# Hymba layer on one core: SyncE's requests for the MLP's rows move ahead of the writes of the block before

## The chip, the core and the metric

The kernel runs on one core of a Trainium2 chip. The metric is the device time of one execution in microseconds (us); the time before is the median of three runs. All work is in float32, with matmul operands split in a high and a low part (three products stand for one). TensorE (PE) multiplies and transposes, VectorE (DVE) and ScalarE (ACT) do elementwise work and empty PSUM, GpSimd (POOL) does small work and issues some transfers, SyncE (SP) issues most transfers. Each engine works through its own list in order; a SyncE instruction that has to wait for data or for a free buffer holds up what stands behind it in SyncE's list.

## The reference

One layer of a decoder: two mixers side by side (sliding-window attention and a gated short convolution) and then an MLP with a squared ReLU. 2048 positions, width 1024, MLP width 4096.

```python
h = rms_norm(x, attn_norm_g[l])
z = h @ w_in[l]                       # q, k, v, gate_b, gate_c, xc by columns
y_attn = swa_sink_attention(rms_norm(q, q_norm_g[l]), rms_norm(k, k_norm_g[l]), v, sinks[l])
y_conv = gate_b * short_conv(gate_c * xc, conv_w[l])
y = concatenate([rms_norm(y_attn, attn_out_g[l]), rms_norm(y_conv, conv_out_g[l])])
x = x + y @ w_out[l]
hm = rms_norm(x, mlp_norm_g[l])
x = x + square(relu(hm @ w_up[l])) @ w_down[l]
```

## The kernel before

**Stages.** The mixers run over four chunks of 512 positions (`NCHUNK`, chunk 0 to 3); each chunk's result, the rows x1, is stored to `x1_dram` (L1027). The MLP follows, with its up product (L1514) and its down product (L1631). Both of the MLP's products are done by a scheme of seven block products in place of eight (`ORDER`), which needs sums and differences of blocks of the input. These are the seven planes `xop_dram` that `x_put` (L326 and following) writes.

**The blocks.** The first half of the positions (chunks 0 and 1) is made ready for the MLP while TensorE still works on the last chunk's convolution. This is `x_blocks`. It has `NT` = 4 blocks. Block `t` holds two tiles of 128 rows by 1024 columns: rows of chunk 0 and the same rows of chunk 1. For each block SyncE requests both tiles from `x1_dram` (L351). After three pauses (`X_WAIT`), ScalarE scales a tile by its norm (L357), TensorE transposes it in two halves (L363) through the only PSUM bank with the tag "tr", and VectorE empties the bank with the gain (L364), back into the same tile. Three of the resulting four pieces are written out as they are (L373, the write itself at L334). Four differences are then made in place by VectorE (L377), each over a piece that an earlier write or difference still reads, and each is written too (L378). That is seven writes of 256 KB for a block, against two requests of 512 KB.

**The buffers.** The eight tiles take turns in buffers of the mixers: block 0 the two "xt", block 1 "gb" and one "x1", block 2 two "x1", block 3 one "x1" and again the first "xt". The four "x1" buffers hold the rows of chunk 2 before, and those of chunk 3 (loaded at L1056) afterwards. "gb" holds a gain row of the attention's norm until the last chunk's input is made.

**The order of the work.** `x_blocks` is a generator. `besides` goes one pause further in it at every second step of `conv_pair` (`X_EVERY`), so a block's 12 pauses are spread over the convolution's products. The program order so written is not yet an engine's order: a planner ranks all instructions by their place in the program, shifted in places by `tc.high_priority(offset=...)` (here `ahead(12)` and `ahead(13)`), and simulates the program; each engine takes, of the instructions that are ready at a moment of that simulation, the one that ranks first. An instruction that needs a buffer is ready when the buffer is free in the simulation. `tc.issue_after` pins the transposes behind the latest product. The engine lists that come out of it are fixed when the kernel is built.

Of the kernel before, what the change touches and what calls it, by code (L numbers as in the profile page):

```python
# [36 lines left out]
NT = CH // P  # L37
# [57 lines left out]
def hymba_layer(  # L95
# [50 lines left out]
    def bank(tag, name):  # L146
        return psum.tile([P, 512], F32, tag=tag, name=name, bufs=BANKS[tag])

    def row(tag, name, bufs, dt=F32):

        return pool.tile([P, D], dt, tag=tag, name=name, bufs=bufs)
# [35 lines left out]
    def ahead(i):  # L187

        offset = PRIO[stage[0]][i]
        return tc.high_priority(offset=offset) if offset else nullcontext()  # L190
# [137 lines left out]
    def x_put(tb, t, i, b):  # L328

        dst = xop_dram[tb][ORDER.index(i)]  # L330
        if tb:
            nc.sync.dma_start(dst[:, t * BW : (t + 1) * BW], b)
        else:
            nc.sync.dma_start(  # L334
                dst.rearrange("p (h t c) -> p h t c", h=2, t=NB)[:, :, t], b.rearrange("p (h c) -> p h c", h=2)
            )

    def rs_out(c):

        nc.gpsimd.dma_start(  # L340
            rs_dram[c].rearrange("(p t) -> p t", p=P), rs_x1[:, c * NT : (c + 1) * NT]
        )

    def x_blocks():

        for t in range(NT):
            tags = (("xt", 2), ("xt", 2), ("gb", 1), *((("x1", NT),) * 4), ("xt", 2))[2 * t : 2 * t + 2]
            rows = [row(tag, f"xt_m{c}_{t}", bufs) for c, (tag, bufs) in enumerate(tags)]
            for c, xt in enumerate(rows):
                r = (c * NT + t) * P  # L350
                nc.sync.dma_start(xt, x1_dram[r : r + P, :])  # L351
            for _ in range(X_WAIT):
                yield
            for c, xt in enumerate(rows):
                r = c * NT + t
                with ahead(12):
                    nc.scalar.activation(xt, xt, AF.Copy, scale=rs_x1[:, r : r + 1])  # L357
                for k in range(2):
                    with ahead(12), tc.issue_after(last_sum[0]):
                        pt = bank("tr", f"pt_m{c}_{t}_{k}").rearrange("p (j q) -> p j q", j=NB)  # L360
                        b = xt[:, k * BW : (k + 1) * BW]
                        for j in range(NB):
                            nc.tensor.transpose(pt[:, j], b[:, j * P : (j + 1) * P], ident)  # L363
                        nc.vector.tensor_tensor(  # L364
                            b.rearrange("p (j q) -> p j q", j=NB),
                            pt,
                            g_cols[:, k * NB : (k + 1) * NB, None].to_broadcast([P, NB, P]),
                            op=ALU.mult,
                        )
                    yield  # L370
            b11, b21, b12, b22 = (xt[:, k * BW : (k + 1) * BW] for xt in rows for k in range(2))
            for i, b in ((3, b22), (1, b11), (2, b21)):
                x_put(0, t, i, b)  # L373
            yield
            for i, dst, a, b in ((5, b11, b12, b11), (7, b12, b22, b12), (6, b22, b22, b11), (4, b21, b21, b22)):
                with ahead(13):
                    nc.vector.tensor_tensor(dst, a, b, op=ALU.subtract)  # L377
                    x_put(0, t, i, dst)  # L378
                yield

    def merged(dst, *planes):

        pairs = dst.bitcast(U16).rearrange("p k (t i) -> p i k t", i=2)
        for i, plane in enumerate(planes):
            nc.vector.tensor_copy(pairs[:, i], plane)
# [9 lines left out]
    def prepare(src, r0, gb, dst, name):  # L395
# [29 lines left out]
        def whole(t):  # L425
            with ahead(9), behind():
                for n, raw in enumerate(places[t]):
                    merged(
                        raw.rearrange("p (k t) -> p k t", k=KH), *(turned_[t][:, i, n * KH : (n + 1) * KH] for i in range(2))
                    )  # L430
# [245 lines left out]
    with tc.tile_pool(name="mix_small", bufs=1) as mix_small, tc.tile_pool(name="mix", bufs=1) as mix:  # L676
# [60 lines left out]
        def qk_transpose(b, zt):  # L737

            nm = f"b{b}"
            own = b % 2  # L740
            lo, hi = slice(0, DH), slice(DH, P)
            sc = mix.tile([P, HEADS, P], F32, tag="sc", name=f"sc_{nm}", bufs=2) if b >= TURN_Q else None
            qt = mix.tile([P, HEADS // 2, 2, P], F32R, tag="qt", name=f"qt_{nm}", bufs=1)
            if b >= TURN_Q:
                turned_z = zt[:, :O_V].bitcast(U16).rearrange("p (i n t) -> p i n t", i=2, t=P)
                with ahead_z(2):
                    merged(sc[:, : O_V // P], turned_z[:, 0], turned_z[:, 1])
                p3, pk = sc[:, :4], sc[:, 4]
            else:
                pt = bank("at", f"ptq_{nm}")  # L750
                for j in range(4):
                    nc.tensor.transpose(pt[:, j * P : (j + 1) * P], zt[:, j * P : (j + 1) * P], ident)
                pk = bank("at", f"ptk_{nm}")[:, :P]
                nc.tensor.transpose(pk, zt[:, O_K:O_V], ident)
                p3 = pt.rearrange("p (j q) -> p j q", j=4)
            for i, (a, o) in enumerate(((lo, hi), (hi, lo))):
                nc.scalar.copy(qt[a, :, i, :], p3[a])
                nc.vector.tensor_tensor(qt[o, :, i, :], p3[a], qt[a, :, i, :].bitcast(F32), op=ALU.subtract)
                nc.scalar.copy(kw[a, i, i, own, :], pk[a])
                nc.scalar.copy(kw[o, 1 - i, i, own, :], pk[a])  # L760
                nc.vector.tensor_tensor(kw[o, i, i, own, :], pk[a], kw[a, i, i, own, :].bitcast(F32), op=ALU.subtract)
                nc.vector.tensor_tensor(
                    kw[a, 1 - i, i, own, :], pk[a], kw[a, i, i, own, :].bitcast(F32), op=ALU.subtract
                )
            return qt, sc
# [217 lines left out]
        def out_projection(c, half, ys, rs, x1):  # L983

            for dh in range(2):
# [11 lines left out]
                for t, i in order:  # L997
# [21 lines left out]
                    with ahead(11):  # L1019
                        nc.vector.scalar_tensor_tensor(  # L1020
                            x1[t][:, cs], ps, rs[:, t : t + 1], x1[t][:, cs], op0=ALU.mult, op1=ALU.add
                        )
                        if dh and not half:
                            r = (c * NT + t) * P

                            eng = nc.gpsimd if c + 1 == NCHUNK else nc.sync
                            eng.dma_start(x1_dram[r : r + P, :], x1[t])  # L1027

                            if c + 1 < NCHUNK:
                                norm_stats(x1[t], f"m{c}_{t}", rs_x1[:, c * NT + t : c * NT + t + 1])  # L1030
                                if t + 1 == NT and c == NCHUNK - 2:
                                    rs_out(c)
                    yield

        def besides(c, before, h, yt, rc, x1, h_next, z_next):

            yield from before
            ssc = mix.tile([P, CH], F32, tag="ssc", name=f"ssc{c}", bufs=1)
            blocks = x_blocks() if c + 1 == NCHUNK else None
            if c + 1 < NCHUNK:  # L1040
                steps = prepare(xf, (c + 1) * CH, g_row[0], h_next, f"a{c + 1}")
# [263 lines left out]
    def prepare_rest():  # L1305

        c = NCHUNK - 1
        for t in range(NT):
# [4 lines left out]
            norm_stats(xt, nm, rs_x1[:, r // P : r // P + 1], junk=piece("st", f"junk_{nm}"))  # L1313
            yield
        rs_out(c)
        rows = pool.tile([P, 2, BW], F32, tag="xt", name="rs_rest", bufs=2)
        for i in range(2):
# [353 lines left out]
```

## Time and profile before

| What | Value |
|---|---|
| Time, median of 3 runs | 1910.71 us (1909.95 to 1911.93) |
| Profiled execution's own time | 1909.29 us |
| Its span, first to last instruction | 1907.6 us |
| TensorE busy | 1895.1 us (99%) |
| VectorE busy | 1230.1 us (64%) |
| ScalarE busy | 868.5 us (46%) |
| HBM read and written | 286.35 MB and 125.83 MB |
| Requests of the blocks (L351) | 8 transfers, 468.8 to 569.1 us |
| Writes of the blocks (L334) | 28 transfers, 553.1 to 636.6 us |
| Transposes of the blocks (L363) | 64, 550.5 to 626.8 us |

Times inside the profile are counted from the start of the span. A row of a timeline gives the start, the length, the engine, the line of the kernel, the operation with output and input, the number of instructions merged in it, and in brackets the engine's idle time before it and what ended that. "SPq" is SyncE's queue of transfers. In a table of stretches each engine has its busy time and number of instructions, and at the end stand the granted clock of TensorE, the busy share of the DMA engines and the rate in GB/s. The span and the launch around it differ by 1.69 us in the profiled execution.

### The profile page before, as it was taken

The numbers are of one execution on the slowest core, as the hardware profiler recorded it, in microseconds if no ns is written. First come the engines' busy times: TensorE is split into PE (matmuls) and PEld (weight loads), VectorE is DVE, ScalarE is ACT, GpSimd is POOL, SyncE is SP. The second block draws the span as 40 slices with busy tenths as digits, with TensorE's granted clock in tenths as the row PEclk, the third lists the DMA queues.
The fourth block names the chain that finished last, engine by engine and source line by source line (L and its number), as shares of the span: only waits on it lengthen the run. The fifth ranks groups of instructions, "written<-read, shape, count | busy, mean of one in ns | idle before, by whom it ended". The sixth has DMA issues, their size and how long they took to land.

```text
span 1907.6 us, 24456 instructions
## 1 busy us (share of the span) xinstructions
PE 1895.1 (99%) x8774; PEld 1574.3 (83%) x8774; DVE 1230.1 (64%) x1929; ACT 868.5 (46%) x1605; POOL 291.2 (15%) x477
## 2 busy tenths in 40 slices
PE   9999999999999999999999999999999999999999
PEld 8878887888877888888888888888888888888887
DVE  5886577568568759998788766666534334447441
ACT  6656356456554445545565545463322232222220
POOL 2213213322221112233111101011000000100000
PEclk9999999999999999999999999999999999999999
DMA  8997965667687688777575544448954456776541
GB/s 294 336 293 200 330 243 198 213 241 233 206 304 254 225 295 250 230 211 248 201 242 197 176 140 161 138 155 320 367 194 144 144 168 225 280 230 210 186 158 55
DMA packets 273690, 424.03 MB, mean 222 GB/s; under 512 B 92568, under 2 KB 177312, under 8 KB 260768
## 3 DMA queue, kind: packets, MB, share of 16 engines
q1 hardware_dynamic: 244736, 346.82, 55.5%
q0 software_dynamic: 15424, 51.40, 6.9%
q10 hardware_dynamic: 13408, 24.26, 3.4%
q8 instruction: 69, 1.13, 0.2%
q14 instruction: 53, 0.43, 0.1%
HBM read 286.35 MB, written 125.83 MB: 216 GB/s over the span
## 4 chain that ended last, share of the span: by engine, by line
PE 47%; issue 5%; POOL 1%; DMA 0%; DVE 0%; DVEq 0%; POOLq 0%
PE d L1631 32%; PE u L1514 15%; POOL fop L1250 1%; DMA fop<-s 0%; POOL st_m L1188 0%; DVE wop L492 0%; DVE d L1574 0%; DVE op_x L473 0%; POOLq L1250 0%; DVEq L1666 0%; DVE s L1253 0%; DVEq L1253 0%; DVEq L492 0%; DVEq L473 0%
## 5 line engine op out<-in xcount | busy, mean ns | idle before, releaser
L1514 PE MATMUL u<-op_x,wop 128*128 128x512 f32 x2688 | 609.8, 389 | 0.5 <-DVE wop L492 0.5
L1631 PE MATMUL d<-op_w,op_f 128*128 128x512 f32 x2691 | 609.5, 389 | 0.0
L1514 PEld LDWEIGHTS u<-op_x,wop 128*128 128x128 f32 x2688 | 504.3, 188 | 105.8 <-DVE wop L492 0.9
L1631 PEld LDWEIGHTS d<-op_w,op_f 128*128 128x128 f32 x2691 | 504.8, 188 | 104.7
L473 DVE TENSOR_TENSOR op_f<-op_f 128x1024 fp32r<-128x1024 f32 x112 | 136.9, 1225 | 236.7 <-ACT op_f L472 236.5
L472 ACT CAST op_f<-op_f 128x1024 fp32r<-128x1024 f32 x112 | 117.7, 1052 | 354.1 <-DMA op_f<-fop 341.0
L491 ACT CAST wop<-wu 128x512 fp32r<-128x512 f32 x156 | 96.1, 619 | 89.1 <-PE u L1514 86.7
L492 DVE TENSOR_TENSOR wop<-wu,wop 128x512 fp32r<-128x512 f32 x156 | 110.4, 710 | 31.4 <-DMA wu<-in_w_up_dram 20.1
L1250 POOL DMA_DIRECT2D fop<-s x96 | 52.1, 542 | 443.5 <-DVE s L1253 439.1
L1256 DVE TENSOR_TENSOR u<-u,u 128x512 f32<-128x512 f32 x128 | 87.9, 687 | 18.6 <-PE u L1514 18.3
L473 DVE TENSOR_TENSOR op_w<-raw,op_w 128x1024 fp32r<-128x1024 f32 x56 | 68.3, 1222 | 23.6 <-ACT op_w L472 23.4
L472 ACT CAST op_w<-raw 128x1024 fp32r<-128x1024 f32 x56 | 58.8, 1052 | 44.0 <-DVE raw L1461 20.3
L828 POOL TENSOR_SCALAR_AFFINE_SELECT pp_b<-pp_b 128x512 fp32r<-128x512 f32 x60 | 46.5, 785 | 140.3 <-ACT pp_b L821 86.9
L1262 ACT ACTIVATE u<-u 128x512 f32<-128x512 f32 x64 | 40.5, 632 | 58.6 <-DVE u L1256 56.3
L796 ACT ACTIVATE sc_b<-sc_b,ngm_b 128x128 f32<-128x128 f32 x128 | 49.6, 389 | 22.6 <-DVE ngm_b L793 22.5
L1463 POOL DMA_DIRECT2D wds<-raw x16 | 8.5, 533 | 329.3 <-DVE raw L1461 329.3
L492 DVE TENSOR_TENSOR wop<-wu_s,wop 128x512 fp32r<-128x512 f32 x64 | 46.0, 720 | 11.9 <-ACT wop L491 11.8
L491 ACT CAST wop<-wu_s 128x512 fp32r<-128x512 f32 x64 | 39.4, 619 | 30.2 <-PE u L1514 24.5
L281 PE MATMUL pout<-w_wo,yt_c 128*128 128x512 f32 x128 | 50.7, 397 | 0.8 <-DVE x L1020 0.7
L281 PE MATMUL pb_c<-h_a,w_wb 128*128 128x512 f32 x128 | 51.2, 400 | 0.0
L282 PE MATMUL pout<-w_wo,yt_c 128*128 128x512 f32 x128 | 50.6, 396 | 0.4 <-DVE w_wo L254 0.4
L281 PE MATMUL pc_c<-h_a,w_wc 128*128 128x512 f32 x128 | 50.9, 398 | 0.1
(249 smaller groups left out, 3141.5 us busy)
## 6 DMA issues: line engine op xcount, KB each, us to landing
op_f<-fop SPq DMA_DIRECT2D x112, 512.0 KB, 4.3
raw<-in_w_down_dram SPq DMA_DIRECT2D x72, 512.0 KB, 4.3
wu<-in_w_up_dram SPq DMA_DIRECT2D x128, 256.0 KB, 4.3
w_wo<-wo SPq DMA_DIRECT2D x24, 1024.0 KB, 7.3
fop<-s POOLq DMA_DIRECT2D x96, 256.0 KB, 2.7
fop<-u ACTq DMA_DIRECT2D x64, 256.0 KB, 2.4
op_x<-xop SPq DMA_DIRECT2D x28, 512.0 KB, 6.3
w_q<-q SPq DMA_DIRECT2D x12, 1024.0 KB, 5.6
```

Of the source, the lines that this page charges most:

```text
L281: nc.tensor.matmul(ps, st(0), mv(0), start=first, stop=False)
L282: nc.tensor.matmul(ps, st(0), mv(1), start=False, stop=False)
L472: nc.scalar.copy(op[:, 0], raw)
L473: nc.vector.tensor_tensor(op[:, 1], raw, op[:, 0].bitcast(F32), op=ALU.subtract)
L491: splits.append(nc.scalar.copy(hi, blk).ins)
L492: lows.append(nc.vector.tensor_tensor(lo, blk, hi.bitcast(F32), op=ALU.subtract).ins)
L796: nc.scalar.activation(sc[:, hd, :], sc[:, hd, :], AF.Exp, bias=ngm[:, hd : hd + 1], accum_out=den[:, hd : hd + 1])
L828: nc.gpsimd.affine_select(part, full, pattern=[[0, GQ], [1, P]], compare_op=ALU.is_ge, fill=0.0, base=0, channel_multiplier=-1,)
L1250: eng.dma_start(fop_dram[tb][ORDER_DOWN.index(i)][n // 2][:, n % 2], b)
L1256: return nc.vector.tensor_tensor(dst, ps, b, op=ALU.add).ins
L1514: nc.tensor.matmul(pt, wops[i][:, a, k, :], xops[tb, p][k // 2][:, b, k % 2, :], start=p not in GOES_ON and k + j == 0, stop=k + j == NB + ...
L1631: nc.tensor.matmul(ps[tb][j][:, cs], fs[tb][:, a, k, j * P : (j + 1) * P], w[:, b, k, cs], start=first and p not in GOES_ON and k + n == 0 ...
```

## The change

The request of a block becomes a function, `request(t)`. Block 0's is made before the loop. In block `t`, when its first tile is turned and before its second tile is scaled, the request of block `t + 1` is written; the block's seven writes come after it in the program. Before, the request of block `t + 1` stood after block `t`'s last write. What a block requests, its tags, its buffers and its pauses stay. Two more lines of the diff remove empty lines.

```diff
     def x_blocks():
-
-        for t in range(NT):
+        def request(t):
             tags = (("xt", 2), ("xt", 2), ("gb", 1), *((("x1", NT),) * 4), ("xt", 2))[2 * t : 2 * t + 2]
             rows = [row(tag, f"xt_m{c}_{t}", bufs) for c, (tag, bufs) in enumerate(tags)]
             for c, xt in enumerate(rows):
                 r = (c * NT + t) * P
                 nc.sync.dma_start(xt, x1_dram[r : r + P, :])
+            return rows
+
+        ahead_rows = request(0)
+        for t in range(NT):
+            rows = ahead_rows
             for _ in range(X_WAIT):
                 yield
             for c, xt in enumerate(rows):
+                if c and t + 1 < NT:
+                    ahead_rows = request(t + 1)
                 r = c * NT + t
                 with ahead(12):
                     nc.scalar.activation(xt, xt, AF.Copy, scale=rs_x1[:, r : r + 1])
...
```

## The prediction

> **What bounds the kernel now.** I read the page's first part for the engine that sets the end, then TensorE's busy time stage by stage, to see how much a better order could win at all.
>
> ```profile
> span 1907.6 us, 24456 instructions
> PE 1895.1 (99%) x8774; PEld 1574.3 (83%) x8774; DVE 1230.1 (64%) x1929; ACT 868.5 (46%) x1605; POOL 291.2 (15%) x477
> ...
> core 0: us, PE busy (x) PEld busy (x) DVE busy (x) ACT busy (x) POOL busy (x), PEclk, DMA share, GB/s
> 543.00:561.00 18.00, 17.43 (x99) 14.37 (x98) 10.88 (x26) 14.32 (x40) 3.68 (x10) 1.00 1.03 347
> 561.00:593.00 32.00, 29.95 (x157) 24.57 (x156) 29.92 (x71) 20.88 (x63) 6.49 (x10) 1.00 0.74 264
> 593.00:626.00 33.00, 32.64 (x165) 27.05 (x164) 27.21 (x56) 11.99 (x33) 4.92 (x8) 1.00 0.81 274
> ...
> 640.00:700.00 60.00, 60.00 (x276) 49.68 (x275) 33.45 (x53) 20.23 (x34) 9.21 (x26) 1.00 0.74 251
> 700.00:1000.00 300.00, 300.00 (x1325) 248.40 (x1324) 260.78 (x372) 166.94 (x277) 67.34 (x90) 1.00 0.74 233
> ```
>
> TensorE is idle for 1907.6 - 1895.1 = 12.5 us of the whole span, at a granted clock of 1.00. The blocks that the change touches are turned between 543 and 626 us. There TensorE is idle for 18.00 - 17.43 = 0.57, 32.00 - 29.95 = 2.05 and 33.00 - 32.64 = 0.36 us: 2.98 us together. From 640 to 1000 us it is never idle, so nothing that these blocks hand on to the MLP is late at present. What the change can win on TensorE's idle time is at most 2.98 us, 0.16% of the time.
>
> Next I read SyncE's queue in order of time, for the requests (L351) and the writes (L334). A row may hold several transfers in a row; its second number then includes the waits between them.
>
> ```profile
> start us, us, engine line op out<-in xcount [idle before <-releaser]
> 468.81 0.33 SPq L351 DMA_DIRECT2D xt_m<-x_dram  x1
> ...
> 487.61 0.32 SPq L351 DMA_DIRECT2D xt_m<-x_dram  x1
> ...
> 547.34 0.57 SPq L1027 DMA_DIRECT2D x_dram<-x  x1
> 548.02 0.38 SPq L351 DMA_DIRECT2D xt_m<-x_dram  x1
> 548.82 1.87 SPq L242 DMA_DIRECT2D w_wb<-wb  x2
> 553.14 2.80 SPq L334 DMA_DIRECT2D xop<-xt_m  x2
> 556.03 1.16 SPq L351 DMA_DIRECT2D xt_m<-x_dram  x2
> 558.52 3.76 SPq L334 DMA_DIRECT2D xop<-xt_m  x3
> ...
> 565.16 2.24 SPq L334 DMA_DIRECT2D xop<-xt_m  x2
> ...
> 568.14 1.26 SPq L351 DMA_DIRECT2D xt_m<-x_dram  x2
> ...
> 576.34 2.38 SPq L334 DMA_DIRECT2D xop<-xt_m  x2
> ```
>
> This is the view that decides for me. Each block has two rows, so the requests come in pairs: block 0's first row at 468.81, block 1's two at 487.61 and 548.02, block 2's pair at 556.03, block 3's pair at 568.14. Each block has seven writes. Block 0's are the two at 553.14, the three at 558.52 and the two at 565.16, seven in all; block 1's begin at 576.34. So block 1's requests (548.02 the later) already stand ahead of block 0's first write (553.14), and those of blocks 2 and 3 (556.03, 568.14) ahead of block 1's first (576.34), and so of block 2's. In the text of the kernel each request stands behind the preceding block's writes; in the queue that the planner made of it, none does.
>
> **The change part by part.** No instruction is added or removed. Six transfers of 512 KB (two rows for each of blocks 1, 2 and 3) move forward in the program from the head of their own block to the middle of the block before, between its first row's and its second row's turning. A block's turning is spread over 12 pauses and the request moves forward by 7 of them. The rows of TensorE's transposes price that distance.
>
> ```profile
> 553.17 0.66 PE L363 MATMUL pt_m<-ident,xt_m 128*128 128x128 f32 x4 [0.46 <-DVE xt_m L364]
> ...
> 572.32 0.60 PE L363 MATMUL pt_m<-ident,xt_m 128*128 128x128 f32 x4
> ...
> 576.37 0.66 PE L363 MATMUL pt_m<-ident,xt_m 128*128 128x128 f32 x4 [2.05 <-DVE xt_m L364]
> ...
> 597.76 0.60 PE L363 MATMUL pt_m<-ident,xt_m 128*128 128x128 f32 x4
> 600.11 0.66 PE L363 MATMUL pt_m<-ident,xt_m 128*128 128x128 f32 x4 [0.36 <-DVE xt_m L364]
> ...
> 618.36 0.60 PE L363 MATMUL pt_m<-ident,xt_m 128*128 128x128 f32 x4
> ```
>
> Blocks 1 and 2 start to be turned at 572.32 and 597.76, 25.4 us apart, so 7 of 12 pauses are 14.8 us. That is less than the planner's own lead: block 2's request left at 556.03, 41.7 us ahead of its first transpose, block 3's at 568.14, 50.2 us ahead.
>
> The saving on the way of the data comes first. For a request to matter, the scaling on ScalarE (L357), which waits for it, must hold up the transposes.
>
> ```profile
> 553.81 1.15 ACT L357 ACTIVATE xt_m<-xt_m,rs_x 128x1024 f32<-128x1024 f32 x1 [2.11 <-issue]
> ...
> 562.17 1.15 ACT L357 ACTIVATE xt_m<-xt_m,rs_x 128x1024 f32<-128x1024 f32 x1 [1.64 <-DMA xt_m<-x_dram]
> ...
> 563.96 1.16 ACT L357 ACTIVATE xt_m<-xt_m,rs_x 128x1024 f32<-128x1024 f32 x1
> ...
> 575.09 1.15 ACT L357 ACTIVATE xt_m<-xt_m,rs_x 128x1024 f32<-128x1024 f32 x1 [1.63 <-DMA xt_m<-x_dram]
> ...
> 577.73 1.15 ACT L357 ACTIVATE xt_m<-xt_m,rs_x 128x1024 f32<-128x1024 f32 x1
> ```
>
> Block 1's second row is scaled by 554.96 (553.81 + 1.15), 17.4 us ahead of that block's first transpose; block 2's rows by 565.12, 32.6 us ahead; block 3's by 578.88, 39.5 us ahead. The saving is 0 for all six transfers: the cover is these 17 to 40 us of other products. If the cover were gone, the price would be ScalarE's waits, 1.64 and 1.63 us. None of the three stalls of TensorE (0.46, 2.05, 0.36) names a request; each names VectorE's emptying of the one PSUM bank that all blocks share (L364).
>
> The second part is what the moved transfers do to what they are moved past on SyncE's queue. Going by the text, each request passes seven writes of 256 KB and any weight load placed between. Going by the queue, it passes no write of the preceding block, as shown above. What is left is that the planner ranks the six requests earlier. How early they can go is set by their buffers: block 1's second row, both of block 2's and block 3's first use the four buffers that hold the third chunk's rows, the last of which is only being stored at 547.34; block 3's second row uses block 0's first buffer and cannot be fetched before block 0's writes are out (the last issued in the row at 565.16, the request in the row at 568.14). So block 3 has nothing to gain in that buffer, and block 2 could come forward by at most 556.03 - 548.02 = 8.0 us, into a place ahead of block 0's first write. I take this as not happening, 0 us, because in both programs block 2's request ranks behind block 0's writes: each request changes rank against the one block before it, and is ahead of that block's writes already.
>
> The cost if it does happen can be read from what waits for that first write.
>
> ```profile
> L334 SPq DMA_DIRECT2D xop<-xt_m x1: 615/615/615, 553.1 to 553.1; - x1
> ...
> DMA to landing us min/median/max: 7.1/7.1/7.1
> ...
> 560.32 0.69 DVE L377 TENSOR_TENSOR xt_m<-xt_m,xt_m 128x512 f32<-128x512 f32 x1 [1.83 <-DMA xop<-xt_m]
> ...
> 567.03 0.40 ACT L796 ACTIVATE sc_b<-sc_b,ngm_b 128x128 f32<-128x128 f32 x1 [1.91 <-DVE ngm_b L793]
> ...
> 575.63 0.68 DVE L364 TENSOR_TENSOR xt_m<-pt_m,g_cols 128x512 f32<-128x512 f32 x1
> ...
> 543.00:576.00 33.00, 1.00 1.02 352
> ```
>
> The first write takes 7.1 us to land, in a stretch where the 16 DMA engines are full (share 1.02, 352 GB/s). VectorE's subtraction (L377) overwrites what that write reads, and waits 1.83 us for it. Behind it in VectorE's order stand the softmax pieces for which ScalarE then waits (1.91 us at 567.03), and at the end of that chain the bank at 575.63, for which TensorE waits 2.05 us. This is how a transfer reaches the critical engine here. Two rows of 524288 bytes put ahead of that write take 1.05 MB / 352 GB/s = 3.0 us, so the bounds for this term are +3.0 us (the write lands so much later) and -1.83 us (the earlier request leaves the full stretch to the write and VectorE's wait goes). My value, 0, lies between.
>
> [...]
>
> The third part is the new plan. The planner issues by rank and readiness, and six instructions change rank, so near ties elsewhere in this stretch may fall otherwise. The trace has no row for that. I bound it below by the loss of all idle time in the stretch, -2.98 us, and above by all four blocks stalling like block 1's 2.05 us: 4 x 2.05 - (0.46 + 2.05 + 0.36) = +5.3 us. I take 0, as most of the plan's order is fixed by buffers and by the products.
>
> Sum: 0 + 0 + 0. The profiled execution took 1909.29 us, 1.69 us beside its span of 1907.6; the median of the runs is 1910.71, 1.4 us above that execution. The forecast as a median is 1910.7 us.
>
> **The rivals.** *The requests really come forward and it helps.* For it speaks that ScalarE does wait for block 2's and 3's rows (1.64, 1.63 us) and that the stall of 2.05 us hangs on transfers in a full stretch. Against it speaks that the buffers set the requests' times. The time is 1910.7 - 1.8 = 1908.9 us when VectorE's wait goes, 1907.7 us when every stall of the stretch goes.
>
> *The requests come forward and push the writes back.* The place is block 0's first write; the price is 3.0 us on VectorE's wait at 560.32, which goes through to TensorE one for one since both wait already; it decides as soon as block 2's pair is queued ahead of 553.14. Time 1913.7 us. For it speaks the full DMA stretch, against it the ranks.
>
> *The plan falls worse.* Another order of the softmax, bank and convolution work on VectorE, busy for 29.92 of 32 us in the middle stretch, would stall more blocks: up to 1916.0 us. For it speaks how full that engine is; against it that only six transfers change rank.
>
> *The change doesn't do what it says:* the queue already has this order. That is my forecast, 1910.7 us.
>
> **How the numbers follow.** Forecast 0.58, help 0.16, writes pushed back 0.13, a worse plan 0.13. A measurement of this kernel can tell about 0.2% from no change, 3.8 us: below 1906.9 is faster, above 1914.5 slower. The forecast lies within. The help ends at 1907.7, still within; a third of it, 0.06, goes to faster for orders that also shorten what TensorE counts as busy. The worse plan reaches from 1911 to 1916 and beyond, with 0.09 of its 0.13 above the bound; of the pushed writes, 0.06 lies above it, where the stall repeats. That gives faster 0.06, same 0.79, slower 0.15. The range runs from 1907.0, the help's limit less the spread of the runs, to 1916.0, the worse plan's limit.
>
> **What would show it right or wrong.** Right: SyncE's queue has the eight L351 rows at nearly the same places among the L334 rows, ScalarE scales blocks 2 and 3 tens of microseconds ahead of their transposes, and TensorE's idle time between 543 and 626 us stays near 3 us. Help: VectorE no longer waits at its first L377. Pushed writes: an L351 pair ahead of the first L334 row, whose landing exceeds 7.1 us, and a longer stall before the second transposes of block 1. A worse plan: new stalls of TensorE on VectorE or ScalarE that name no transfer. The forecast is wrong if the request reaches a buffer earlier than I read, or if the stretch's idle time grows past 7 us.

## The result and the profile after

The changed kernel takes 1913.64 us (median of 16 runs, 1912.28 to 1915.53), against 1910.55 us for the kernel before in the same comparison (16 runs, 1907.97 to 1912.01). The ratio is 1.0016 with a 95% interval of 1.001 to 1.0023: 3.1 us slower. That lies inside the predicted range and below the 0.2% that the prediction set as its bound, but the interval leaves 1 out. The forecast of no change at all was wrong, on a small scale. Times are medians; a ratio is estimated from the runs of its comparison, not from the two medians, and can differ from their quotient by some 0.0006.

The span and the engines' busy time from the page of the changed kernel:

```profile
span 1912.3 us, 24455 instructions
PE 1897.7 (99%) x8774; PEld 1574.3 (82%) x8774; DVE 1229.9 (64%) x1929; ACT 868.2 (45%) x1605; POOL 289.1 (15%) x477
```

Its table of stretches, for the three stretches of the prediction and then four slices of 3 us each:

```profile
543.00:561.00 18.00, 14.05 (x64) 11.40 (x64) 7.88 (x21) 11.00 (x32) 3.51 (x9) 0.82 1.01 306
561.00:593.00 32.00, 31.66 (x173) 26.38 (x172) 28.97 (x69) 19.47 (x58) 4.32 (x9) 1.00 0.76 259
593.00:626.00 33.00, 32.58 (x166) 26.93 (x165) 26.64 (x52) 13.60 (x39) 5.15 (x10) 1.00 0.75 256
...
553.00:556.00 3.00, 0.00 (x0) 0.00 (x0) 2.94 (x8) 2.15 (x7) 0.00 (x0) 0.72 0.79 306
556.00:559.00 3.00, 2.77 (x9) 2.38 (x10) 2.63 (x7) 0.40 (x3) 0.00 (x0) 0.50 0.98 402
559.00:562.00 3.00, 3.00 (x13) 2.32 (x12) 0.28 (x1) 2.89 (x16) 0.00 (x0) 0.64 0.83 255
562.00:565.00 3.00, 3.00 (x23) 2.62 (x22) 2.91 (x8) 0.75 (x2) 0.00 (x0) 1.00 0.59 225
```

TensorE's idle time by stretch was 0.57, 2.05 and 0.36 us. It is now 18.00 - 14.05 = 3.95, 32.00 - 31.66 = 0.34 and 33.00 - 32.58 = 0.42 us. So a stall of 3.95 us has come up in the first stretch and the one of 2.05 us in the second has gone: 4.71 us in place of 2.98, +1.7 us. The slices show a second loss that idle time doesn't. After the stall the granted clock is 0.50 and then 0.64, so of the 2.77 and 3.00 us that TensorE is busy there, an estimated 2.77 x 0.50 + 3.00 x 0.36 = 2.5 us are lost to the clock. Its products of 128x512 start 0.43 us apart there (558.00 to 560.56), against 0.23 us ahead of the stall (550.27 to 551.89). Together that is 1.7 + 2.5 = 4.2 us.

A second reckoning agrees. These are the rows of the blocks' 64 transposes, of the kernel before and then of the changed one, with the start of the first and of the last:

```profile
L363 PE MATMUL pt_m<-ident,xt_m x64: 270/272/333, 550.5 to 626.8; 128*128 128x128 f32 x64
```

```profile
L368 PE MATMUL pt_m<-ident,xt_m x64: 270/273/476, 549.6 to 630.0; 128*128 128x128 f32 x64
```

The blocks are turned in 626.8 - 550.5 = 76.3 us before and in 630.0 - 549.6 = 80.4 us after: +4.1 us of the 1912.3 - 1907.6 = 4.7 us between the two spans. This distance, first to last transpose, serves as a gauge below.

Where the stall comes from is read backwards. TensorE's timeline of the changed kernel:

```profile
549.59 0.60 PE L368 MATMUL pt_m<-ident,xt_m 128*128 128x128 f32 x4
...
551.89 0.39 PE L283 MATMUL pc_c<-h_a,w_wc 128*128 128x512 f32 x1
556.23 1.12 PE L368 MATMUL pt_m<-ident,xt_m 128*128 128x128 f32 x4 [3.95 <-DVE xt_m L369]
```

The second transposes of block 0 wait for VectorE to empty the bank (L369) that the first ones filled at 549.59. VectorE's timeline, after and below it before, says why it is late:

```profile
551.57 0.29 DVE L765 TENSOR_TENSOR kw<-sc_b,kw 64x128 fp32r<-64x128 f32 x1 [7.56 <-ACT kw L763]
...
555.49 0.68 DVE L369 TENSOR_TENSOR xt_m<-pt_m,g_cols 128x512 f32<-128x512 f32 x1
```

```profile
548.26 0.50 DVE L790 COPY_PREDICATED sc_b<-later,psc_b 128x128 f32<-128x128 int32 x2 [3.35 <-ACT sc_b L787]
...
552.42 0.69 DVE L364 TENSOR_TENSOR xt_m<-pt_m,g_cols 128x512 f32<-128x512 f32 x1
```

VectorE has done nothing for 7.56 us: it waits for ScalarE's casts of the attention's operand `kw` (L763). Before, it waited for ScalarE at this place too, but only 3.35 us. The bank's emptying stands behind that work in its list and comes at 555.49, against 552.42 before. ScalarE's timeline, after, and below it the same place before:

```profile
550.20 1.15 ACT L362 ACTIVATE xt_m<-xt_m,rs_x 128x1024 f32<-128x1024 f32 x1 [3.52 <-issue]
551.26 0.28 ACT L763 CAST kw<-sc_b 64x128 fp32r<-64x128 f32 x1
```

```profile
547.85 0.37 ACT L787 COPY sc_b<-psc_b 128x256 f32<-128x256 f32 x1 [0.27 <-PE psc_b L779]
548.21 0.30 ACT L759 CAST kw<-sc_b 64x128 fp32r<-64x128 f32 x1
...
551.33 0.37 ACT L787 COPY sc_b<-psc_b 128x256 f32<-128x256 f32 x1
```

After, ScalarE is idle for 3.52 us ahead of the scaling of a block row (L362) and takes the casts only behind it. Before, the first of the casts and copies started at 547.85 and the last at 551.33, and the scaling (L357 at 553.81) came behind them all. ScalarE's wait is put down to "issue", but the request explains it. SyncE's timeline of the changed kernel, then the landing of the request at 544.83:

```profile
544.83 0.32 SPq L349 DMA_DIRECT2D xt_m<-x_dram  x1
545.26 0.58 SPq L1031 DMA_DIRECT2D x_dram<-x  x1
545.95 2.11 SPq L739 DMA_TRANSPOSE z<-sq_b  x1
548.49 1.50 SPq L242 DMA_DIRECT2D w_wb<-wb  x2
556.20 2.78 SPq L334 DMA_DIRECT2D xop<-xt_m  x2
559.08 1.07 SPq L349 DMA_DIRECT2D xt_m<-x_dram  x2
563.88 1.86 SPq L334 DMA_DIRECT2D xop<-xt_m  x3
568.06 2.24 SPq L334 DMA_DIRECT2D xop<-xt_m  x2
571.05 2.53 SPq L349 DMA_DIRECT2D xt_m<-x_dram  x2
```

```profile
L349 SPq DMA_DIRECT2D xt_m<-x_dram x1: 319/319/319, 544.8 to 544.8; - x1
...
DMA to landing us min/median/max: 5.3/5.3/5.3
```

The request left at 544.83 and landed 5.3 us later, at 550.1; the scaling started at 550.20. The request is that of block 1's second row. It is the only request that moved in SyncE's list; behind it, the chunk's last store and the attention's transposing transfer change places. The lists as built, with the full names of the tiles (`xt_m1_1` is the second row of block 1, `x1_2_3` the last row of chunk 2):

```
before: x1_dram<-x1_2_2;  TRANSPOSE z3_3<-sq_b15;  x1_dram<-x1_2_3;  xt_m1_1<-x1_dram;          w_wb ...
after:  x1_dram<-x1_2_2;  xt_m1_1<-x1_dram;        x1_dram<-x1_2_3;  TRANSPOSE z3_3<-sq_b15;    w_wb ...
```

The five other requests of blocks 1, 2 and 3 keep their places: blocks 2 and 3 are still requested at 559.08 and 571.05, between the same writes as before. What changed is that one request stands ahead of the chunk's last store and of the attention's transposing transfer, and that its consumer stands ahead of the attention's casts in ScalarE's list. The lists of VectorE and TensorE were replanned along with it. The theory that the runs had to test is this: ScalarE, which works in order, waits for a landing while work that is ready stands behind it. The rival is that the transfers themselves cost it, by the new order in SyncE's list or by what the early request takes from others on the full DMA engines (share 1.01).

### The profile page after: what moved, and what is told of

It is laid out like the page before. It is cut to its first block, busy times and chain, and to the rows that moved or that the text cites. A ratio compares the mean times of both kernels' runs of the same rounds, so it can differ in the third digit from the quotient of the medians.

```text
span 1912.3 us, 24455 instructions
## 1 busy us (share of the span) xinstructions
PE 1897.7 (99%) x8774; PEld 1574.3 (82%) x8774; DVE 1229.9 (64%) x1929; ACT 868.2 (45%) x1605; POOL 289.1 (15%) x477
## 4 chain that ended last, share of the span: by engine, by line
PE 47%; issue 5%; POOL 1%; DMA 0%; DVE 0%; DVEq 0%; POOLq 0%
PE d L1635 32%; PE u L1518 15%; POOL fop L1254 0%; DMA fop<-s 0%; POOL st_m L1192 0%; DVE wop L496 0%; DVE op_x L477 0%; DVE f L1257 0%; DVE d L1578 0%; DVEq L1670 0%; POOLq L1254 0%; DVE s L1257 0%; DVEq L477 0%; DVEq L496 0%; DVEq L1257 0%
## 5 line engine op out<-in xcount | busy, mean ns | idle before, releaser
L281 PE MATMUL pc_c<-h_a,w_wc 128*128 128x512 f32 x128 | 51.9, 405 | 0.1
L281 PE MATMUL pout<-w_wo,yt_c 128*128 128x512 f32 x128 | 50.7, 397 | 0.8 <-DVE x L1024 0.7
L282 PE MATMUL pc_c<-h_a,w_wc 128*128 128x512 f32 x128 | 51.2, 400 | 0.0
```

Source lines behind the costliest of these rows:

```text
L281: nc.tensor.matmul(ps, st(0), mv(0), start=first, stop=False)
L282: nc.tensor.matmul(ps, st(0), mv(1), start=False, stop=False)
```

## The experiments

### The scaling alone put back

```diff
-                with ahead(12):
+                with ahead(12), tc.issue_after(casts[-1]) if (c, t) == (1, 1) else nullcontext():
                     nc.scalar.activation(xt, xt, AF.Copy, scale=rs_x1[:, r : r + 1])
...
-                nc.scalar.copy(kw[o, 1 - i, i, own, :], pk[a])
+                casts.append(nc.scalar.copy(kw[o, 1 - i, i, own, :], pk[a]).ins)
```

This is the changed kernel; only the scaling of block 1's second row is held behind the latest of ScalarE's casts.

> All requests as in the changed kernel, but ScalarE's scaling of block 1's second row is issued only behind the casts of the next attention block, where it stood before the change. Theory A (ScalarE waits in order for the early request, and everything behind it is late): ScalarE's wait of 3.5 us ahead of that scaling and TensorE's stall of 3.95 us before block 0's second transposes go, granted clock 1.00 from 543 to 561 us, time 1908 to 1911 us. Rival B (SyncE's queue itself: the attention's transpose and the store behind the request are late): the stall stays, 1913 to 1914 us. Rival C (the later order of VectorE and TensorE, which is new all through the stretch): 1912 to 1914 us with stalls after 561 us.

It took 1909.79 us (11 runs) against 1910.55 (28 runs): ratio 1.0002, 0.9993 to 1.0011. The slowdown is gone. Rows of its timeline (SyncE, ScalarE, TensorE), and below them the first row of its table of stretches:

```profile
544.64 0.32 SPq L350 DMA_DIRECT2D xt_m<-x_dram  x1
545.07 0.99 SPq L1032 DMA_DIRECT2D x_dram<-x  x1
546.17 2.40 SPq L740 DMA_TRANSPOSE z<-sq_b  x1
...
546.94 0.37 ACT L792 COPY sc_b<-psc_b 128x256 f32<-128x256 f32 x1 [0.27 <-PE psc_b L784]
...
550.80 1.15 ACT L363 ACTIVATE xt_m<-xt_m,rs_x 128x1024 f32<-128x1024 f32 x1
...
552.25 0.66 PE L369 MATMUL pt_m<-ident,xt_m 128*128 128x128 f32 x4 [0.46 <-DVE xt_m L370]
```

```profile
543.00:561.00 18.00, 17.54 (x100) 14.75 (x100) 9.82 (x24) 13.41 (x39) 3.53 (x9) 1.00 1.06 322
```

The request still leaves early (544.64), ahead of the store and the transposing transfer, at a DMA share of 1.06. But the scaling, now behind the casts, waits for nothing, TensorE's stall is 0.46 us as before the change, and the clock stays at 1.00 in this stretch. From the request to the scaling it is 550.80 - 544.64 = 6.2 us here. ScalarE spends that time, from 546.94 on, on the casts and copies, while in the changed kernel it stands idle and begins them at 551.26. So that work was ready, and the wait for the landing held it up.

As built, SyncE's list is that of the changed kernel, and the lists of the other engines are those of the kernel before all through this stretch. So the run separates the order of the transfers from the order of the engines: SyncE's order costs nothing; the place of the scaling in ScalarE's list, with what the planner ordered after it, costs it all. No run moves the scaling alone and keeps the new order of VectorE.

### One block's request at a time

```diff
-        ahead_rows = request(0)
+        ahead_rows = {}
...
-            rows = ahead_rows
+            rows = ahead_rows.pop(t, None) or request(t)
...
-                if c and t + 1 < NT:
-                    ahead_rows = request(t + 1)
+                if c and t + 1 == 1:
+                    ahead_rows[t + 1] = request(t + 1)
```

So only block 1 is requested ahead. For blocks 2 and 3 alone the condition reads `t + 1 in (2, 3)`. A third kernel requests only block 1's first row ahead, and its second row, as before the change, at the block's own head.

> Only block 1's request is moved; those of blocks 2 and 3 stand at the head of their blocks as before the change. Theory A and rival B: the whole loss is here, 1913 to 1914.5 us, stall of about 4 us. If the requests of blocks 2 and 3 carry the loss: 1910 to 1911 us.

> Block 1's request stands where it stood before the change; those of blocks 2 and 3 are moved. Theory A and rival B: no loss, 1910 to 1911.5 us, no stall above 2.1 us. If blocks 2 and 3 carry the loss: 1913 to 1914 us.

> Of all requests only that of block 1's first row is moved. Its buffer was free long before, so theory A and rival B expect no loss: 1909.5 to 1911.5 us, no stall above 2.1 us. If the moved rank alone costs time through a new order: 1912 to 1914 us.

Block 1 alone took 1915.28 us (6 runs), ratio 1.0029 (1.0018 to 1.0041). Blocks 2 and 3 alone took 1910.68 us (11 runs), ratio 1.0002 (0.9993 to 1.0011). Block 1's first row alone gave the same, 1910.68 us (11 runs), 1.0002 (0.9993 to 1.0011). The whole loss hangs on one transfer, block 1's second row. Why block 1 alone costs more than the whole change (1.0029 against 1.0016) is not known. With block 1 alone, TensorE's waits (in total, times, longest) and the first stretch were:

```profile
PE pt_m L368 <- DVE xt_m L369: 5.5, 3, 4.1
```

```profile
543.00:561.00 18.00, 13.84 (x65) 11.19 (x64) 9.26 (x24) 10.39 (x25) 4.16 (x10) 0.87 0.97 314
```

The longest wait is 4.1 us and the clock falls, as in the changed kernel. In the two kernels without that request the longest waits, 2.5 and 1.8 us, are at block 1, where the kernel before has its 2.05.

### Half the transfer

```diff
-                nc.sync.dma_start(xt, x1_dram[r : r + P, :])
+                cols = slice(0, BW) if (c, t) == (1, 1) else slice(0, D)
+                nc.sync.dma_start(xt[:, cols], x1_dram[r : r + P, cols])
+                if (c, t) == (1, 1):
+                    nc.gpsimd.memset(xt[:, BW:], 0.0)
```

> The changed kernel, but of block 1's second row only the first 512 of 1024 columns are requested; the other half is left out and set to zero by GpSimd (so the MLP's first half of positions gets wrong rows there; the shapes and the work behind it stay). Theory A (the loss is ScalarE's wait for the landing): half the bytes land sooner, by 1 to 2 us, so ScalarE's wait ahead of that scaling falls from 3.5 to 1.5 to 2.5 us and TensorE's stall from 3.95 to 2 to 3 us; if the granted clock falls only after the longer stall, the time is 1910.5 to 1912 us, otherwise 1912 to 1913 us. Rival (the loss is in the new order itself, whatever lands when): stall and time as in the changed kernel, 1913 to 1914 us.

1912.86 us (11 runs) against 1910.85 (33 runs), ratio 1.0009 (1.0 to 1.0018). ScalarE's and TensorE's rows of its timeline:

```profile
549.69 1.15 ACT L365 ACTIVATE xt_m<-xt_m,rs_x 128x1024 f32<-128x1024 f32 x1 [2.45 <-DMA xt_m<-x_dram]
...
555.94 0.66 PE L371 MATMUL pt_m<-ident,xt_m 128*128 128x128 f32 x4 [3.52 <-DVE xt_m L372]
```

Here the profile itself names the request as what ended ScalarE's wait. The wait shrank from 3.52 to 2.45 us, because half the bytes still took 4.3 us to land instead of 5.3. The stall of TensorE shrank less than expected, from 3.95 to 3.52 us, so the size of the transfer is only a small lever on it. The profiled execution is one of the slower ones of this kernel (1915.38 us). SyncE's list is not quite the same either: the transposing transfer stands ahead of the last store here. The time lies between the kernel before and the changed one and its interval touches 1; it settles nothing by itself.

### The stall of 2.05 us at block 1

The prediction read that stall as the end of a chain from a late write of block 0 (VectorE's L377 waits for it). Three kernels hold the first two differences of block 0 back, so that VectorE takes softmax pieces instead of waiting for the write. The first is made on the kernel before, the second on the changed kernel with its scaling put back, the third as the second but one softmax later.

```diff
-                with ahead(13):
+                with ahead(13), tc.issue_after(norms[-2]) if not t and i in (5, 7) else nullcontext():
                     nc.vector.tensor_tensor(...)
...
-            nc.vector.tensor_tensor(sc, sc, den[:, :, None].to_broadcast([P, HEADS, P]), op=ALU.mult)
+            norms.append(nc.vector.tensor_tensor(sc, sc, ...).ins)
```

> The kernel before the change, with the first two differences of block 0 on VectorE queued behind the normalisation of the attention block before (and so no longer waiting first in line for block 0's first write). If TensorE's stall of 2.05 us at block 1 hangs on VectorE's wait for that write, as the prediction read it: VectorE's wait of 1.83 us goes, the stall falls below 1 us, 1908 to 1909.7 us. If the stall hangs on the other work ahead of the bank's emptying: stall 1.8 to 2.5 us, 1910 to 1911 us.

> All requests early as in the changed kernel, the scaling of block 1's second row back at its old place on ScalarE as in the first experiment, and the two differences late as in e6. If the early request as such is worth anything: faster than e6, 1907 to 1909 us. If it is worth nothing: as e6, 1908 to 1909.7 us, or 1910 to 1911 us where e6 gains nothing.

> As e7, with the two differences queued behind the normalisation of the next attention block, so that VectorE has less ahead of block 1's bank. TensorE's stall at block 1 below 0.5 us; 1907.5 to 1909 us if nothing else becomes late; 1911 to 1913 us if the writes that move with the differences hold SyncE's queue up and the last chunk's rows come too late.

On the kernel before: 1907.76 us (11 runs) against 1910.85 (33 runs), ratio 0.9989 (0.998 to 0.9998). On the changed kernel with the scaling back: 1908.94 us (11 runs), 0.9991 (0.9982 to 0.9999). One softmax later: 1913.18 us (11 runs), 1.001 (1.0001 to 1.0019). VectorE's wait for the write is gone, and the first two gain a little. But the stall is not gone in the profile. TensorE's waits and the middle stretch of the first:

```profile
PE pt_m L364 <- DVE xt_m L365: 2.9, 3, 2.1
```

```profile
561.00:593.00 32.00, 29.90 (x148) 24.46 (x147) 27.82 (x65) 19.16 (x58) 6.31 (x10) 0.95 0.68 251
```

The longest wait is 2.1 us, as before, with the clock at 0.95. The profiled execution is the slowest of the 11 (1911.76 us), so it may not stand for the others. Rows of ScalarE and VectorE show what took the place of the write:

```profile
562.73 1.15 ACT L358 ACTIVATE xt_m<-xt_m,rs_x 128x1024 f32<-128x1024 f32 x1 [2.12 <-DMA xt_m<-x_dram]
563.79 0.35 ACT L788 COPY sc_b<-psc_b 128x256 f32<-128x256 f32 x1
```

```profile
564.17 0.50 DVE L791 COPY_PREDICATED sc_b<-later,psc_b 128x128 f32<-128x128 int32 x2 [2.06 <-ACT sc_b L788]
```

ScalarE's scaling of block 2's first row waits 2.12 us for its landing, the attention's copy stands behind it, and VectorE waits 2.06 us for that copy in place of 1.83 us for the write. It is the mechanism of the changed kernel, on a smaller scale and on the kernel before: there the same scaling waits 1.64 us at 562.17. So the run swapped one wait of VectorE for another, and does not tell what the stall hangs on; why the first two kernels are faster is not settled either. The third, with the differences held back longest, has four waits of 4.1 us in all.

### The same two kernels again

> The kernel before, unchanged, for a second profile. If the granted clock falls after a stall only in some executions (the stall of 2.05 us at block 1 left it at 1.00 in the first profile, stalls of 1.85 and 2.5 us in other kernels took it to 0.5): either the same as the first profile, stall 1.8 to 2.5 us and clock 1.00, or the same stall with some 2 us more between 575 and 582 us at a clock near 0.5. Every stretch ahead of 543 us within 1 us of the first profile.

> The changed kernel, unchanged, for a second profile. If the stall of 3.95 us takes the clock down each time: ScalarE waits 3 to 4 us, TensorE's stall is 3.5 to 4.2 us, then 4 to 5 us at a clock near 0.5, span 1910 to 1913 us. If the low clock there is a chance as in block 1: clock 1.00 and 2 us less.

One more execution of each: 1911.6 us before, 1915.68 us after. This is the stall at block 1 in the timeline of the kernel before, in this execution, and below it the slice behind it:

```profile
575.49 1.01 PE L363 MATMUL pt_m<-ident,xt_m 128*128 128x128 f32 x4 [2.12 <-DVE xt_m L364]
```

```profile
577.00:580.00 3.00, 3.00 (x11) 2.30 (x11) 2.51 (x5) 2.12 (x4) 1.65 (x3) 0.66 0.71 225
```

In its first profile the same slice stood at full clock:

```profile
577.00:580.00 3.00, 3.00 (x17) 2.48 (x16) 3.00 (x7) 2.13 (x4) 1.86 (x3) 1.00 0.69 245
```

With the same instructions and almost the same stall (2.12 and 2.05 us), the clock fell once and once it didn't. The blocks took 78.0 us from first to last transpose here against 76.3: 1.7 us more. So the first profile, against which the idle time and the clock of the changed kernel were set above, shows the kernel before in a lucky execution. The changed kernel again, its stall in the timeline and the slices around it:

```profile
557.54 1.11 PE L368 MATMUL pt_m<-ident,xt_m 128*128 128x128 f32 x4 [4.42 <-DVE xt_m L369]
```

```profile
556.00:559.00 3.00, 1.46 (x6) 1.37 (x7) 2.94 (x8) 0.50 (x2) 0.00 (x0) 0.53 0.90 374
559.00:562.00 3.00, 3.00 (x9) 2.32 (x8) 0.98 (x4) 2.09 (x11) 0.00 (x0) 0.50 0.56 175
```

Stall and low clock are both back, and the blocks took 81.3 us. From the four profiles the difference is 80.4 - 78.0 = 2.4 us at least and 81.3 - 76.3 = 5.0 us at most; the 3.1 us between the medians lies between.

### One more pause ahead of block 1's next piece

```diff
                 for k in range(...):
...
+                    if (c, t, k) == (0, 1, 0):
+                        for _ in range(1):
+                            yield
```

The second transposes of block 1's first row come one pause later, so that VectorE has more time to empty the bank. Once on the kernel before alone, once together with the two differences held back.

> The kernel before with one more pause between the transposes of the two halves of block 1's first row, which puts eight more products of the convolution (1.8 us) ahead of the second transposes. If the stall at block 1 is TensorE's early arrival at the shared bank: it falls from 2.05 to under 0.6 us, and with it the chance of the low clock: 1907.5 to 1909.5 us. If other work becomes late in its place: 1910 to 1912 us.

> As e11, and the two first differences of block 0 late as in e6. The two help at the same place: 1907 to 1909 us, stall at block 1 under 0.5 us; slower than 1910 us if the order that comes out makes another bank late.

The pause alone took 1909.88 us (11 runs) against 1910.89 (21 runs), ratio 0.9996 (0.9987 to 1.0005): the stall at block 1 went, but 1.4 us of a wait came up at another product (L1072). Both together took 1907.61 us (11 runs, 1905.71 to 1908.73), ratio 0.9984 (0.9975 to 0.9993), faster than both kernels. The middle stretch and the row of the transposes:

```profile
561.00:593.00 32.00, 31.65 (x164) 26.06 (x163) 30.17 (x66) 22.79 (x68) 8.41 (x11) 1.00 0.73 258
```

```profile
L364 PE MATMUL pt_m<-ident,xt_m x64: 270/272/331, 549.6 to 624.7; 128*128 128x128 f32 x64
```

The idle time of the middle stretch is 0.35 us in place of 2.05, at full clock, and the blocks take 75.1 us. The gain of 3.3 us is larger than that stretch's 1.7 us. The profiled execution is the fastest of the 11, and the rest may be the low clock that followed this stall in some executions; no run separates that.

## Why the prediction was right and wrong

**The bound, and the saving of 0: right.** No transpose had waited for a request, and none gained: block 1's second row is scaled 3.6 us earlier (550.20 against 553.81), which no stall of TensorE repays.

**"The queue already has this order": right for five requests of six.** They kept their places among the writes, as the SyncE rows show. The run with blocks 2 and 3 alone, 1.0002, is what the forecast described.

**The step that failed is "moved past", 0 us.** It said that each request changes rank against the block before it alone, and is ahead of that block's writes already. That looked only at writes of the blocks. In the program the requests also stand between the instructions of the convolution and the attention, and block 1's second row changed rank against those: it passed the third chunk's last store and the attention's transposing transfer. The second half of the error is the cover. The prediction asked only whether the scaling comes too late (17.4 us ahead, so no) and named as the price of lost cover ScalarE's waits, 1.64 and 1.63 us. It did not ask what an earlier scaling is put ahead of. A request that leaves earlier makes its consumer ready earlier in the planner's simulation, and the planner then places it earlier in an engine that works in order. (What landing time the planner reckons with is not on record; that it was too short is inferred from where it put the scaling.) On the chip the landing took 5.3 us. ScalarE waited 3.52 us for it with ready casts behind it, and VectorE (7.56 us) and TensorE (3.95 us) waited in turn. The first experiment shows this: with the scaling put back and the request still early, the time is that of the kernel before.

**What made room for the move was a buffer that the prediction misread.** The prediction took the third chunk's last store, at 547.34, for what frees the four buffers. As built, block 1's second row uses the buffer of the chunk's first row, which is stored first. In the changed kernel that store left at 538.5 and landed 6.2 us later, at 544.7, and the request left at 544.83. The prediction had named this as a sign of a wrong forecast: the request reaches a buffer earlier than it read.

**"New plan", 0 with bounds of -2.98 and +5.3 us: the bounds held, the value did not.** The sign and kind were those of the rival "the plan falls worse": a new stall of TensorE on VectorE that names no transfer. Its price was put together from stalls of 2.05 us; the real one is 3.95 us in one place, and the old one at block 1 went, +1.7 us of idle time. **A term was missing:** the clock behind a stall, an estimated 2.5 us, more than the 1.7 us by which idle time grew. The other sign set for a wrong forecast, idle time past 7 us in this stretch, was not reached (4.71 us), since idle time shows only part of this loss.

**The rival "pushed writes" gave 1913.7 us, the time measured, by a mechanism that did not happen: luck.** No pair of requests stood ahead of block 0's first write, and the changed kernel's VectorE no longer waits for that write at its first difference (the write landed in 4.2 us, against 7.1 before). The 3.0 us were the author's estimate: that a write lands later by the time of the bytes put ahead of it was not shown by any run. What the runs show is the early request of the first experiment: put ahead of a store and a transposing transfer, it cost nothing (1.0002), so here the order in SyncE's queue did not set the time.

**The reading of the 2.05 us stall was not confirmed.** Take away VectorE's wait for the write, and a stall of 2.1 us stands in the one profile taken, but with a wait of 2.06 us for ScalarE in the write's place. So it was not refuted either.

**What stays open.** Some 0.6 us of the difference between the two spans lies outside the blocks, and no run traces it. Why holding the differences back gains 0.1%, when the one profile still has the stall, was not found.

## What to carry to other kernels

When a request is moved forward, look for its consumer in the list of an in-order engine: a planner that thinks the data ready earlier hoists the consumer too, and if the landing takes longer than planned, what is ready behind it waits (here ScalarE's casts, for 3.52 us). Ask of every moved instruction which instructions of other work it changes places with, not only those named in the change. In these traces a stall of TensorE of 3.95 us cost an estimated 2.5 us more by the clock behind it; look at the granted clock in short slices, since such a loss hides in busy time.

## What the runs showed of the hardware that was not expected

The granted clock fell behind each of the four stalls of 3.5 us or more that the profiles show at the blocks. In the two slices of 3 us from 556 to 562 us it then stood at 0.50 and 0.64 (3.95 us), at 0.55 and 0.50 (4.1 us, block 1 alone), at 0.53 and 0.50 (4.42 us) and at 0.70 and 0.73 (3.52 us). Behind the shorter stall at block 1 it fell in six of the eight profiles that have one. Behind 1.85, 2.1, 2.12, 2.3 and 2.5 us it stood between 0.50 and 0.66 in the slice from 577 to 580 us; behind 1.7 us the mean of the middle stretch is 0.95, as in those five. Behind 1.8 and 2.05 us it stayed at 1.00. So at these lengths the length of the stall alone doesn't decide, and the first profile of the kernel before is one of the two exceptions. With the scaling put back there was a stall of 1.85 us at block 1; its row of the timeline, and the slice behind it:

```profile
575.97 0.94 PE L369 MATMUL pt_m<-ident,xt_m 128*128 128x128 f32 x4 [1.85 <-DVE xt_m L370]
```

```profile
577.00:580.00 3.00, 3.00 (x9) 2.31 (x9) 3.00 (x6) 2.12 (x4) 1.91 (x3) 0.56 0.73 243
```

The clock was 0.56 there, against 1.00 in the same slice behind the longer stall of 2.05 us. What decides whether the clock falls behind stalls of 1.7 to 2.5 us, no run here shows.
